# An inference step of a two-layer hybrid backbone: tensor-tensor work taken from POOL to DVE, and four adaLN segments of the second layer made in that layer

## The chip, the core and the metric

The kernel runs on one core of one Trainium2 chip. The metric is the device time of one execution in microseconds (us); the median of three timed runs of the kernel before is 1954.43 us (1951.92 to 1954.71). All times below are of that core. Its engines are PE (matrix multiplication), DVE and ACT (elementwise work on 128 partitions; DVE also reduces), POOL (GpSimd, elementwise too) and SP, which issues all of the kernel's DMAs.

## The reference, cut to what matters

512 latent tokens and 128 context tokens, 1024 channels, two layers (DEPTH), float32. In each layer a vector of six modulation segments is made from the conditioning vector and used for both norms and both residual additions:

```python
mod = jax.nn.silu(cvec) @ p['w_ada'] + p['b_ada']
sh1, sc1, g1, sh2, sc2, g2 = jnp.split(mod, 6, axis=-1)
h = rmsnorm(x, p['norm1_g']) * (1 + sc1) + sh1
out, k, v = mixer(h, p, rope, ctx_kv)       # pooling, gated conv and attention; three gates; w_o
x = x + g1 * out
h2 = rmsnorm(x, p['norm2_g']) * (1 + sc2) + sh2
ffn = (jax.nn.silu(h2 @ p['w_gate']) * (h2 @ p['w_up'])) @ p['w_down']
x = x + g2 * ffn
```

Latent and context tokens have their own conditioning vector (`c` and `c_ctx`), so that each segment exists twice. `w_ada` has 1024 x 6144 weights per layer.

## The kernel before

Channels lie on partitions, tokens on columns: a tensor of 1024 channels is eight chunks of 128 x 640 (KC = 8, TOK = 640), which PE works on in two halves of 320 columns. Float32 products are made of rounded parts: every operand is split into `hi` (ACT rounds it) and `lo` (an elementwise engine subtracts), and PE adds up hi*hi, lo*hi and hi*lo. So every weight block that arrives by DMA costs ACT one copy (L351) and one subtraction on DVE (L355) or POOL (L353), in `half_split`, and so does every activation (`split`, L297 to L301). A `Unit` is such a weight block; `stream` loads them in the order in which PE takes them.

The stages of a layer, in order: first norm; keys, values, queries, pooling and convolution projections with attention beside them ("attention stage"); 24 merges of a gate, a branch projection and their product (`gate`, L1484 to L1502, "gate stage"); the output projection `w_o` with the residual and the second norm (`residual`, `norm_chunk`); the FFN in four groups. Most FFN weight blocks go through `Pair` and `Seven`, which make a product of two 2 x 2 blocks by seven multiplications and need sums of weight blocks (`sums`, L446) and of activations (`combine`, L544). `hidden_of` (L1922 to L1931) turns the result into hidden activations, which a down-projection then takes.

The adaLN segments: in the first layer, segments 0 and 1 (shift and scale of the first norm) are made at the very start. All others come from `ada_back`: each 128-channel block of a segment is two jobs of 512 columns; a job loads 256 KB of `w_ada` into one of two buffers `p`, and DVE runs one reduction of 512 columns per conditioning vector (`ttr`, L756), which the profile shows as two instructions, a custom one and the read of its accumulator. The conditioning vectors stand in tiles `k`, which the keys of attention use before.

The order of all engines' instructions is written down by a plan: generators (tasks) yield operations with costs (L261 to L278) and a slack, and `_Order.run` takes for each engine the operation that is due first. For an operation that two engines can do (`dve_pool`) `_Order.push` takes the one that, by these costs, ends it first. On the chip each engine runs its list strictly in that order and waits on semaphores. `ttr` has the slack BACK (1e7 ns), so that the plan puts it where it believes DVE to be free; `quiet` keeps it out while a norm is made.

Names that the text uses: L353 and L355 weight subtractions; L446 sums of weight blocks; L902 the multiplication of a chunk by the norm's factor, L924 and L926 its affine step on ACT and DVE, L948 the subtraction that yields its low part; L849 the sum of squares; L651 the addition of a PSUM result to an accumulator in `Seven`; L300 and L301 the split of hidden activations and merged gates; L1489 and L1495 the products and sums of the merges; L885 and L1030 powers (x to -0.5), which POOL alone does.

## Time and profile before

| | |
|---|---|
| median of 3 runs | 1954.43 us (1951.92 to 1954.71) |
| profiled execution | 1951.29 us, its span 1949.2 us |
| PE busy | 1849.3 us (95%) |
| DVE busy | 1460.6 us (75%) |
| ACT busy | 795.3 us (41%) |
| POOL busy | 307.9 us (16%) |
| SP | issues the DMAs: 195.81 MB, mean 100 GB/s |

Stages of the profiled execution, by the places where the chain of waits changes its lines: start to 64 us; first layer's attention to 235.3, its gates to about 476 and output projection to 519.6, second norm to 585, FFN to about 990; norm between the layers to 1040; second layer's attention to 1200, gates and output projection to 1473.7, norm to 1538.2, FFN to 1929.2; the final norm to 1949.2.

How to read it: PE's busy time includes pipelined matmuls whose ends are modelled. An engine's wait is put down to what released it last. An idle engine off the path costs nothing, and a busy share of the whole span hides that the first layer has adaLN work and the second none.

### The profile page before, as it was taken

To read this page: it belongs to the slowest core of one execution; us is meant where nothing else is said; L and a number is where in the kernel's file an instruction comes from. 1 tells how busy PE (TensorE), PEld (TensorE's weight loads), DVE (VectorE), ACT (ScalarE), POOL (GpSimd) and SP (SyncE) were. 2 spreads that over 40 slices of the span, in tenths; PEclk is the share of its full clock that TensorE was granted. 3 is DMA by queue.
4 is the path that set the end of the run, shared out by engine and by line. 5 is a ranking of instruction groups with operands and counts; after the bars stand their busy time and mean duration, and the time that the engine had idled before them with its cause. 6 is when DMAs were issued, how large, how long until landed. Compare 5 with 4: busy or idle time off the path is not lost.

```text
span 1949.2 us, 31521 instructions
## 1 busy us (share of the span) xinstructions
PE 1849.3 (95%) x12427; PEld 1806.2 (93%) x12427; DVE 1460.6 (75%) x2529; ACT 795.3 (41%) x1396; POOL 307.9 (16%) x246
## 2 busy tenths in 40 slices
PE   6999999998989999999988999999998999999997
PEld 4889999998979999999988889999998899999997
DVE  7699778888889998997777996333347957768575
ACT  5476622222344242342454675222224534425244
POOL 3333000000341010100135320000004301001011
PEclk9999999999999999999999999999999999999998
DMA  8211144446314434433242100222241122222222
GB/s 303 77 35 40 39 151 158 169 161 227 114 33 133 155 112 159 136 129 107 69 161 60 35 29 33 77 82 76 76 141 55 52 90 76 87 76 79 84 71 71
DMA packets 76533, 195.81 MB, mean 100 GB/s; under 512 B 8801, under 2 KB 12897, under 8 KB 76385
## 3 DMA queue, kind: packets, MB, share of 16 engines
q1 hardware_dynamic: 76386, 193.81, 29.9%
q8 instruction: 97, 1.59, 0.3%
q14 instruction: 50, 0.41, 0.1%
HBM read 186.96 MB, written 5.51 MB: 99 GB/s over the span
## 4 chain that ended last, share of the span: by engine, by line
PE 63%; DVE 26%; issue 5%; DMA 3%; ACT 3%; POOL 1%; SPq 0%; DVEq 0%; ACTq 0%; POOLq 0%
PE ps L686 41%; PE ps L589 16%; DVE junk L756 5%; DVE wq L355 5%; DMA p<-in_w_ada 2%; DVE g L298 1%; PE ps L1209 1%; PE ps L1247 1%; PE ps L1227 1%; DVE u L446 1%; DVE g L301 1%; DVE g L948 1%; DVE st L1215 1%; DVE g L926 1%; PE ps L1682 1%
## 5 line engine op out<-in xcount | busy, mean ns | idle before, releaser
L686 PE MATMUL ps<-g,wq 128*128 128x320 f32 x7488 | 1153.9, 311 | 18.6 <-ACT g L300 10.1
L686 PEld LDWEIGHTS ps<-g,wq 128*128 128x128 f32 x7488 | 1112.7, 189 | 25.8 <-ACT g L300 11.7
L589 PE MATMUL ps<-g,wq 128*128 128x320 f32 x3360 | 502.7, 311 | 16.5 <-DVE z L651 13.9
L589 PEld LDWEIGHTS ps<-g,wq 128*128 128x128 f32 x3360 | 497.1, 189 | 21.1 <-DVE z L651 17.6
L355 DVE TENSOR_TENSOR wq<-wr,wq 128x512 fp32r<-128x512 f32 (+2 forms) x289 | 266.4, 922 | 157.3 <-ACT wq L351 156.1
L351 ACT CAST wq<-wr 128x512 fp32r<-128x512 f32 (+2 forms) x312 | 244.6, 784 | 311.9 <-PE ps L686 228.9
L1534 DVE SCALAR_TENSOR_TENSOR g<-ps,mod,g 128x128 f32<-128x128 f32 (+3 forms) x172 | 83.5, 522 | 120.7 <-PE ps L686 120.5
L756 DVE CUSTOM_DVE_ANT_0 junk<-p,k,vec 128x512 f32<-128x512 f32 x160 | 129.8, 811 | 29.5 <-DMA p<-in_w_ada 26.3
L351 ACT CAST wq<-u 128x512 fp32r<-128x512 f32 x160 | 98.3, 620 | 118.8 <-PE ps L589 61.9
L756 DVE CUSTOM_DVE_ANT_0 junk<-p,k,part 128x512 f32<-128x512 f32 x160 | 124.3, 777 | 19.2 <-DMA p<-in_w_ada 16.6
L355 DVE TENSOR_TENSOR wq<-u,wq 128x512 fp32r<-128x512 f32 x160 | 117.2, 737 | 16.5 <-ACT wq L351 16.5
L1484 ACT ACTIVATE t<-ps 128x640 f32<-128x640 f32 x32 | 22.6, 706 | 197.0 <-PE ps L686 197.0
L446 POOL TENSOR_TENSOR u<-u,wr 128x512 f32<-128x512 f32 x23 | 34.3, 1493 | 404.8 <-DVE u L446 403.4
L849 POOL TENSOR_TENSOR u<-u,t 128x320 f32<-128x320 f32 x11 | 14.8, 1351 | 429.2 <-ACT t L844 429.2
L353 POOL TENSOR_TENSOR wq<-wr,wq 128x1024 fp32r<-128x1024 f32 x23 | 57.6, 2505 | 109.2 <-ACT wq L351 99.2
L686 PE MATMUL ps<-g,g 128*128 128x320 f32 x192 | 46.7, 360 | 21.3 <-DVE g L948 18.6
L1217 ACT ACTIVATE p<-ps,st 128x640 f32<-128x640 f32 x64 | 50.9, 796 | 35.9 <-DVE st L1215 26.3
L924 ACT ACTIVATE g<-t,mod,gain 128x128 fp32r<-128x128 f32 (+4 forms) x96 | 50.9, 576 | 31.9 <-DVE gain L1695 14.6
L298 DVE TENSOR_TENSOR g<-ps,g 128x640 fp32r<-128x640 f32 (+1 forms) x68 | 54.9, 809 | 10.5 <-ACT g L297 9.9
L686 PEld LDWEIGHTS ps<-g,g 128*128 128x128 f32 x192 | 33.4, 212 | 30.1 <-DVE g L948 25.2
L902 POOL TENSOR_TENSOR t<-g,u 128x320 f32<-128x320 f32 (+1 forms) x41 | 53.8, 1320 | 39.8 <-ACT u L970 9.0
L297 ACT CAST g<-ps 128x640 fp32r<-128x640 f32 (+1 forms) x68 | 46.5, 686 | 26.5 <-PE ps L1227 21.9
(172 smaller groups left out, 1702.5 us busy)
## 6 DMA issues: line engine op xcount, KB each, us to landing
p<-in_w_ada SPq DMA_DIRECT2D x160, 256.0 KB, 2.8
wr<-in_w_in SPq DMA_DIRECT2D x76, 512.0 KB, 3.3
wr<-in_w_gate SPq DMA_DIRECT2D x44, 512.0 KB, 3.3
wr<-in_w_up SPq DMA_DIRECT2D x44, 512.0 KB, 3.3
wr<-in_w_down SPq DMA_DIRECT2D x48, 384.0 KB, 3.1
g<-in_w_ada SPq DMA_DIRECT2D x16, 512.0 KB, 7.2
wr<-in_w_br SPq DMA_DIRECT2D x32, 256.0 KB, 2.7
wr<-in_w_o SPq DMA_DIRECT2D x16, 512.0 KB, 4.3
```

Of the source, the lines that this page charges most:

```text
L298: yield dve(n, lambda: nc.vector.tensor_sub(lo, src, hi))
L351: yield act(n, lambda: nc.scalar.copy(hi, src), slack=WEIGHT)
L353: yield pool(n, lambda: nc.gpsimd.tensor_sub(lo, src, hi), slack=WEIGHT)
L355: yield dve(n, lambda: nc.vector.tensor_sub(lo, src, hi), slack=WEIGHT)
L446: f = lambda e: e.tensor_tensor(p[q], p[x], p[y], op=op)
L589: nc.tensor.matmul(out, lhsT=wt[q][:, k * P : k * P + P], rhs=x.get(t, lo, k), start=start and k == 0 and i == 0, stop=stop and k == 3 and ...
L686: nc.tensor.matmul(toks(ps, c0, n), lhsT=wt[:, c], rhs=xt[:, c0 : c0 + n], start=start and i == 0, stop=stop and i == 2,)
L756: return dve(n + 60, lambda: nc.vector.tensor_tensor_reduce(out=waste[:, :n], in0=w, in1=s, scale=0.5, scalar=start, op0=ALU.mult, op1=ALU ...
L902: f = lambda e: e.tensor_mul(t[:, :n], xk, r)
L924: nc.scalar.activation(out, sl, AF.Identity, bias=bias, scale=scale)
L1217: yield act(TOK + 140, lambda: nc.scalar.activation(pp, toks(ps), AF.Exp, bias=st[:, 0:1], accum_out=st[:, 1:2]))
L1534: yield dve(n, lambda: nc.vector.scalar_tensor_tensor(xs, toks(ps, s0, n), mods[l][:, v, seg * KC + m : seg * KC + m + 1], xs, op0=ALU.mul ...
```

## The change

1. Every operation that DVE or POOL could do (`dve_pool`) becomes one that DVE alone does (`dve_any`), and the places with a fixed share for POOL (`back` weight units, the first norm's multiplications, two of eight chunks of the final norm) go to DVE. POOL keeps the powers, the edge factors of the pooling mixer and memsets.
2. `ada_back` is started in each layer's gate stage: in the first layer it makes that layer's segments 2 to 5 and the second layer's segments 0 and 1 (48 blocks), in the second layer that layer's segments 2 to 5 (32 blocks). Before, all 80 blocks belonged to the first layer. The plan holds a norm until the two segments that it reads are made.

```diff
-    def dve_pool(n, f, **kw):
-        return _Op({"dve": 1.04 * n + 75, "pool": 2.2 * n + 100}, lambda e: f(ENG[e]), bias=BIAS, **kw)
+    def dve_any(n, f, **kw):
+        return dve(n, lambda: f(nc.vector), **kw)
...
-    def half_split(hi, lo, src, n, back=False):
+    def half_split(hi, lo, src, n):
         yield act(n, lambda: nc.scalar.copy(hi, src), slack=WEIGHT)
-        if back:
-            yield pool(n, lambda: nc.gpsimd.tensor_sub(lo, src, hi), slack=WEIGHT)
-        else:
-            yield dve(n, lambda: nc.vector.tensor_sub(lo, src, hi), slack=WEIGHT)
+        yield dve(n, lambda: nc.vector.tensor_sub(lo, src, hi), slack=WEIGHT)
...
-                yield dve_pool(n, f, slack=4.0 * WEIGHT)
+                yield dve_any(n, f, slack=4.0 * WEIGHT)
...
-    def ada_back(keys_free):
+    def ada_back(keys_free, todo):
...
-        todo = [(0, 2 * KC + (m + 0)) for m in range(4 * KC)] + [(1, m) for m in range(NADA)]
         jobs = [(l, m, q) for l, m in todo for q in range(2)]
...
         f = lambda e: e.tensor_mul(t[:, :n], xk, r)
-        if first:
-            yield pool(n, lambda: f(nc.gpsimd))
-        else:
-            yield dve(n, lambda: f(nc.vector)) if psum else dve_pool(n, f)
+        yield dve(n, lambda: f(nc.vector))
...
         yield h.made
+        for sg in (3 * which, 3 * which + 1):
+            yield ada_done[l][sg]
...
-        if k in (2, 5):
-            yield copied
-            yield pool(n, lambda: nc.gpsimd.tensor_mul(xk, xk, r_sb))
-        else:
-            yield dve(n, lambda: nc.vector.tensor_mul(xk, xk, r_ps))
+        yield dve(n, lambda: nc.vector.tensor_mul(xk, xk, r_ps))
...
-            bg = None
-            if l == 0:
-                bg = spawn(ada_back(att.done))
+            todo = [(l, m) for m in range(2 * KC, NADA)]
+            todo += [(l + 1, m) for m in range(2 * KC) if l + 1 < DEPTH]
+            bg = spawn(ada_back(att.done, todo))
```

The ten other uses of `dve_pool` change in the same way as the one in `sums`.

The first place is DVE's list at the first layer's second norm, where its second token half begins. Before (multiplication L902, affine step L926, subtraction L948; `msn` the mean squares, `t` the products):

```order
L883 TENSOR_SCALAR msn_84<-ps_5301 128x3
L902 TENSOR_TENSOR t_5324<-g_4627,ps_5301 128x320
L902 TENSOR_TENSOR t_5330<-g_4627,u_4630 128x320
L926 TENSOR_SCALAR g_4634<-t_5324,gain_76,mod_74 128x192
L926 TENSOR_SCALAR g_4634<-t_5324,gain_76,mod_74 128x128
L926 TENSOR_SCALAR g_4634<-t_5330,gain_76,mod_74 128x192
L948 TENSOR_TENSOR g_4632<-g_4634,g_4629 128x320
L926 TENSOR_SCALAR g_4634<-t_5330,gain_76,mod_74 128x128
L926 TENSOR_SCALAR g_4634<-t_5331,gain_76,mod_74 128x192
L948 TENSOR_TENSOR g_4632<-g_4634,g_4629 128x320
```

The same place after; the lines of the steps are now L897, L918 and L940:

```order
L878 TENSOR_SCALAR msn_84<-ps_5300 128x3
L897 TENSOR_TENSOR t_5322<-g_4614,ps_5300 128x320
L897 TENSOR_TENSOR t_5328<-g_4614,u_4617 128x320
L897 TENSOR_TENSOR t_5329<-g_4614,u_4617 128x320
L918 TENSOR_SCALAR g_4621<-t_5322,gain_76,mod_74 128x192
L918 TENSOR_SCALAR g_4621<-t_5322,gain_76,mod_74 128x128
L918 TENSOR_SCALAR g_4621<-t_5328,gain_76,mod_74 128x192
L940 TENSOR_TENSOR g_4619<-g_4621,g_4616 128x320
L897 TENSOR_TENSOR t_5347<-g_4614,u_4617 128x320
L918 TENSOR_SCALAR g_4621<-t_5328,gain_76,mod_74 128x128
L918 TENSOR_SCALAR g_4621<-t_5329,gain_76,mod_74 128x192
L940 TENSOR_TENSOR g_4619<-g_4621,g_4616 128x320
```

Before, DVE multiplied two of the eight chunks of this half and POOL the other six; after, all eight stand in DVE's list, three ahead of the first affine step and then one by one between the others.

The second place is DVE's list in the second layer's gate stage. Before (weight subtractions L355, products L1489, sums L1495, a merge's low part L301):

```order
L355 TENSOR_TENSOR wq_12564<-wr_12418,wq_12563 128x512
L1489 SCALAR_TENSOR_TENSOR t_12562<-t_12562,ps_12558 128x640
L1495 TENSOR_TENSOR u_12321<-u_12321,t_12562 128x640
L355 TENSOR_TENSOR wq_12596<-wr_12440,wq_12595 128x1024
L301 SCALAR_TENSOR_TENSOR g_12139<-u_12321,g_12137 128x640
L355 TENSOR_TENSOR wq_12656<-wr_12491,wq_12655 128x1024
```

After (L352, L1479, L1485 and L301 are the same steps; L752 is the reduction, `ISA` both its instructions):

```order
L1479 SCALAR_TENSOR_TENSOR t_12249<-t_12249,ps_12244 128x640
L752 ISA junk,mod_75<-p_12265,k_11994,part 128x512
L752 ISA mod_75 128x1
L1485 TENSOR_TENSOR u_11884<-u_11884,t_12249 128x640
L352 TENSOR_TENSOR wq_12289<-wr_12115,wq_12288 128x1024
L301 SCALAR_TENSOR_TENSOR g_11956<-u_11884,g_11954 128x640
L752 ISA junk,mod_75<-p_12265,k_12093,part 128x512
L752 ISA mod_75 128x1
L752 ISA junk,part<-p_12284,k_11953,vec 128x512
L752 ISA part 128x1
L752 ISA junk,part<-p_12284,k_12051,vec 128x512
L752 ISA part 128x1
```

Some six reductions now stand in each merge of the second layer, between the steps that the merge itself needs; before there were none.

## Rows read from the trace of the kernel before

**Rows 1.** The page, busy us of each engine (share of span), instructions
```profile
PE 1849.3 (95%) x12427; PEld 1806.2 (93%) x12427; DVE 1460.6 (75%) x2529; ACT 795.3 (41%) x1396; POOL 307.9 (16%) x246
```

**Rows 2.** Stages: stretch, length, each engine's busy us (instructions), clock, DMA share, GB/s
```profile
64.00:235.30 171.30, 163.78 (x1176) 159.26 (x1175) 145.93 (x251) 109.45 (x212) 48.27 (x47) 0.99 0.13 40
235.30:519.60 284.30, 275.84 (x1858) 273.60 (x1858) 225.70 (x458) 69.74 (x98) 19.89 (x10) 0.99 0.50 168
519.60:585.00 65.40, 54.08 (x333) 50.93 (x332) 58.76 (x88) 34.65 (x63) 30.00 (x23) 0.95 0.12 41
585.00:990.00 405.00, 390.18 (x2603) 384.82 (x2604) 362.54 (x712) 151.75 (x266) 41.31 (x28) 0.99 0.39 128
990.00:1040.00 50.00, 42.66 (x268) 40.32 (x266) 38.96 (x72) 26.57 (x53) 27.16 (x19) 0.93 0.33 106
1040.00:1200.00 160.00, 148.66 (x1055) 142.82 (x1056) 141.09 (x238) 103.12 (x203) 41.75 (x46) 0.99 0.13 39
1200.00:1473.70 273.70, 273.70 (x1870) 273.70 (x1869) 99.37 (x118) 68.34 (x94) 6.18 (x4) 1.00 0.26 87
1473.70:1538.20 64.50, 54.11 (x334) 50.78 (x334) 58.65 (x88) 34.62 (x63) 30.35 (x23) 0.94 0.13 42
1538.20:1929.20 391.00, 390.54 (x2643) 390.01 (x2643) 271.88 (x416) 161.09 (x283) 36.43 (x27) 0.99 0.24 76
```

**Rows 3.** PE's waits, first layer's gates: what waited, releaser: us, times, longest
```profile
PE ps L686 <- ACT g L300: 5.1, 1, 5.1
PE ps L686 <- DVE wq L355: 2.9, 4, 1.7
```

**Rows 4.** PE's waits in the first layer's FFN, same columns
```profile
PE ps L589 <- DVE z L651: 10.5, 11, 3.3
PE ps L686 <- ACT g L300: 4.8, 4, 2.0
```

**Rows 5.** AdaLN reductions, line L756: DVE busy by stretch; durations ns min/median/max
```profile
235.30:519.60 284.30, 137.45 (x340) 0.99 0.50 168
585.00:990.00 405.00, 119.10 (x300) 0.99 0.39 128
...
L756 DVE CUSTOM_DVE_ANT_0 junk<-p,k,vec x160: 736/752/2069, 258.5 to 891.7; 128x512 f32<-128x512 f32 x160
```

**Rows 6.** The chain that ended last: start us, length us, what
```profile
76.99 2.55 POOL wq L353
235.29 135.52 PE ps L686 x924
```

**Rows 7.** Groups, shapes apart: line, what, count, busy us, mean ns, idle before
```profile
L355 DVE TENSOR_TENSOR wq<-wr,wq 128x1024 fp32r<-128x1024 f32 x73 | 89.7, 1229 | 49.5 <-ACT wq L351 48.7
L353 POOL TENSOR_TENSOR wq<-wr,wq 128x1024 fp32r<-128x1024 f32 x23 | 57.6, 2505 | 109.2 <-ACT wq L351 99.2 <-DVE st L1220 8.8 <-POOL u L1383 0.7
L902 POOL TENSOR_TENSOR t<-g,u 128x320 f32<-128x320 f32 x33 | 37.6, 1144 | 27.1 <-ACT u L970 9.0 <-DVE g L926 6.2 <-ACT g L924 5.6
L1923 DVE SCALAR_TENSOR_TENSOR t<-t,t 128x640 f32<-128x640 f32 x40 | 46.3, 1157 | 7.2 <-ACT t L1922 7.2
L1489 DVE SCALAR_TENSOR_TENSOR t<-t,ps 128x640 f32<-128x640 f32 x32 | 26.1, 816 | 11.7 <-PE ps L686 11.7
L446 DVE TENSOR_TENSOR u<-wr,wr 128x512 f32<-128x512 f32 x23 | 22.9, 996 | 0.0
L446 DVE TENSOR_TENSOR u<-wr 128x512 f32<-128x512 f32 x33 | 22.6, 686 | 1.0 <-DMA wr<-in_w_up 0.7
L651 DVE TENSOR_TENSOR t<-t,ps 128x320 f32<-128x320 f32 x80 | 38.6, 482 | 6.1 <-PE ps L589 4.3
L1030 POOL TENSOR_TENSOR msz<-msz,mhalf 128x10 f32<-128x10 f32 x10 | 21.3, 2127 | 12.3 <-DVE msz L1028 12.3
```

**Rows 8.** Instructions in order of time, POOL's and DVE's: start us, us, what
```profile
371.81 2.42 POOL L1495 TENSOR_TENSOR u<-u,t 128x640 f32<-128x640 f32 x1 [27.25 <-DVE t L1489]
...
372.73 2.06 DVE L756 CUSTOM_DVE_ANT_0 junk<-p,k,vec 128x512 f32<-128x512 f32 x1
```

More of the change, by code (lines that the diff above doesn't have):

```diff
@@ L362, in tile_backbone, with __init__ @@
     class Unit:
-        def __init__(self, src, n=D, back=False, gate=None, big=False):
-            self.src, self.n, self.back, self.gate, self.big = src, n, back, gate, big
+        def __init__(self, src, n=D, gate=None, big=False):
+            self.src, self.n, self.gate, self.big = src, n, gate, big
             self.loaded, self.ready, self.placed = event(), event(), event()
@@ L386, in prepare @@
             s, raw = self.raw[0]
-            yield from half_split(self.hi[:, :n], self.lo[:, :n], raw[:, :n], n, self.back)
+            yield from half_split(self.hi[:, :n], self.lo[:, :n], raw[:, :n], n)
             RAW.put(s)
@@ L459, in free @@
             WQ.put(self.slot[q])
-    BACK_FROM, BACK_M = 2, 0
     SHIFT = 2000.0
@@ L470, in tile_backbone @@
             gate = go_weights[i] if l == 0 and i < 3 else None
-            plan.append(Unit(a[n][l, b], gate=gate, back=i >= max(BACK_FROM, 3 - 3 * l), big=i == 0))
+            plan.append(Unit(a[n][l, b], gate=gate, big=i == 0))
         MERGE = [(0, 0), (0, 1), (1, 0), (1, 1), (0, 2), (1, 2)]
@@ L474, in tile_backbone @@
         for m, b in MERGE:
-            plan.append(Unit(a["w_in"][l, B_G + b * KC + m], back=m < BACK_M and b < 2))
+            plan.append(Unit(a["w_in"][l, B_G + b * KC + m]))
             if b != 1:
@@ L543, in combine @@
                 for c in (slice(0, 2), slice(2, 4)):
-                    yield dve_pool(2 * HA, lambda e: e.tensor_sub(b[q][:, c], b[x][:, c], b[y][:, c]))
+                    yield dve_any(2 * HA, lambda e: e.tensor_sub(b[q][:, c], b[x][:, c], b[y][:, c]))
                 split_up.append(spawn(self.parts(q, b[q])))
@@ L849, in add @@
                     f = lambda e: e.tensor_add(self.acc[:, c], self.acc[:, c], sq[:, :n])
-                    yield dve_pool(n, f) if k < KC - 3 else dve(n, lambda: f(nc.vector))
+                    yield dve_any(n, f) if k < KC - 3 else dve(n, lambda: f(nc.vector))
                     TT.put(i)
@@ L1058, in rotary @@
         c = spawn(cosine())
-        yield dve_pool(LAT, lambda e: e.tensor_mul(sw[:, :LAT], sw[:, :LAT], rope.t[:, 1, :LAT]))
+        yield dve_any(LAT, lambda e: e.tensor_mul(sw[:, :LAT], sw[:, :LAT], rope.t[:, 1, :LAT]))
         yield c
@@ L1115, in one @@
                 yield dma(hi[r1, PAST:].bitcast(F32), hi[r0, PAST:].bitcast(F32), follow=True, done=d)
-                yield dve_pool(TOK, lambda v: v.tensor_sub(lo[r0, PAST:], z[r0, :], hi[r0, PAST:]))
+                yield dve_any(TOK, lambda v: v.tensor_sub(lo[r0, PAST:], z[r0, :], hi[r0, PAST:]))
                 yield dma(lo[r1, PAST:].bitcast(F32), lo[r0, PAST:].bitcast(F32))
@@ L1178, in one @@
                 yield act(TOK, lambda: nc.scalar.copy(q[r0, :], z[r0, :]))
-                yield dve_pool(TOK, lambda v: v.tensor_sub(q[r1, :], z[r0, :], q[r0, :]))
+                yield dve_any(TOK, lambda v: v.tensor_sub(q[r1, :], z[r0, :], q[r0, :]))
             for d in [spawn(one(e)) for e in range(2)]:
@@ L1368, in pool_mix @@
         lo, hi = 1, POOLW
-        yield dve_pool(POOLW, lambda e: e.tensor_add(cur[:, lo:hi], u[:, lo:hi], u[:, lo - 1 : hi - 1]))
+        yield dve_any(POOLW, lambda e: e.tensor_add(cur[:, lo:hi], u[:, lo:hi], u[:, lo - 1 : hi - 1]))
         step = 1
@@ L1372, in pool_mix @@
             lo, hi = lo + step, hi - step
-            yield dve_pool(POOLW, lambda e: e.tensor_add(
+            yield dve_any(POOLW, lambda e: e.tensor_add(
                 nxt[r, lo:hi], cur[r, lo - step : hi - step], cur[r, lo + step : hi + step]))
@@ L1495, in gate @@
                 f = lambda e: e.tensor_add(acc, acc, t)
-                yield dve_pool(TOK, f) if b == 1 else dve(TOK, lambda: f(nc.vector))
+                yield dve_any(TOK, f) if b == 1 else dve(TOK, lambda: f(nc.vector))
                 TT.put(i)
@@ L1922, in hidden_of @@
         yield act(TOK, lambda: nc.scalar.activation(t, c.x, AF.Tanh, scale=0.5))
-        yield dve_pool(TOK, lambda e: e.scalar_tensor_tensor(t, t, 1.0, c.x, op0=ALU.add, op1=ALU.mult))
+        yield dve_any(TOK, lambda e: e.scalar_tensor_tensor(t, t, 1.0, c.x, op0=ALU.add, op1=ALU.mult))
         TT.put(c.xslot)
         yield c.c22
-        yield dve_pool(HA, lambda e: e.tensor_mul(t[:, HA:], t[:, HA:], c.y))
+        yield dve_any(HA, lambda e: e.tensor_mul(t[:, HA:], t[:, HA:], c.y))
         ZZ.put(c.yslot)
```

## The prediction

> **What bounds the kernel now.** I read the page's busy times first, then the stage table, then who waited for whom on PE. PE is busy for 1849.3 of 1949.2 us and DVE for 1460.6 [rows 1], so only some 100 us of PE idle can be won at all. The stage table shows where they are [rows 2]. The two layers do the same matmuls, so each stage of the first has a twin without adaLN work in the second. The first layer's gate stage with its output projection takes 284.3 us with 8.5 of PE idle, the twin 273.7 with none. The first layer's FFN takes 405 us with 14.8 idle, the twin 391.0 with 0.5. Beside them stand the two attention stages (7.5 and 11.3 idle), the two norms between mixer and FFN (11.3 and 10.4) and the norm between the layers (7.3), where DVE is busy for 78 to 91%.
>
> What PE waits for in the first layer is DVE, or ACT behind it. At the gate stage's end one wait of 5.1 us stands for the last merge, and 2.9 us go to weight halves [rows 3]. In the FFN PE waits 10.5 us for accumulators to be read out (L651) and 4.8 for the hidden tiles (L300) [rows 4]; 3.3 of the 10.5 end just as this stretch begins, and the second layer has the same 3.3. The adaLN instructions keep DVE busy for 137.5 and 119.1 us in these two stretches, and for nothing in the second layer [rows 5].
>
> **The change, part by part.** *AdaLN moved.* Before, 160 jobs of two halves (320 custom reductions) run in the first layer, 153 reductions up to the end of the gates, 17 in the output projection and 150 in the FFN, by the order on DVE. After, the first layer has 96 jobs: 144 to 146 reductions up to the end of the gates, 16 in the projection, 30 in the FFN, the last of them beside the first group's down-projection. The 128 others stand among the second layer's merges 4 to 22 of 24.
>
> FFN of the first layer: 150 reductions become 30. With the twin as the floor, its idle can fall from 14.8 to 0.5. I leave a fifth of it (30 of 150), about 3: a gain of 12, bounds 8 and 14.8. The gate stage of the first layer keeps its load, as adaLN still runs beyond its end: a gain of 1 of the 8.5, bounds -3 and 4.
>
> Gate stage of the second layer: 64 jobs in a stage whose DVE is busy for 99.4 of 273.7 us. At the cost of before (137.5 and 119.1 us for the 320) the 128 reductions add 103 us, which gives DVE 202 of 274, against 225.7 of 284.3 in the first layer. The ends of the unknown are 0 (in the first layer PE ran for 135.5 us from 235.3 on without a stop, with reductions from 258.5 on [rows 5, 6]) and 8.5 (all that the first layer's stage lost). The 5.1 us there came at the end, with reductions still in front of the last merge. Here the last one stands two merges earlier, and DVE can catch up. I take 3. The same stage gets 64 pairs' loads and four loads of the conditioning vectors on SP; the first layer moves 168 GB/s in this stage and no wait of PE there names a DMA. No new wait is late on the chip: the second layer's first two segments are done beside the first of four groups of the first layer's FFN and read after the fourth, and its other four end before the output projection needs the last but one of them.
>
> *POOL's work to DVE.* POOL is busy for 307.9 us [rows 1]; the power operations (21.3 for the ten of L1030 [rows 7]), the edge factors and memsets stay, some 45 us, and about 263 move. On DVE such work takes 1229 ns instead of 2505 for 1024 columns, and 482 instead of 1144 for 320, thus 0.42 to 0.49 of POOL's time: 263 becomes 110 to 129 us, I say 118. By stage, from POOL's busy time less what stays: 15 in the first attention, 14 in the second, 12.6 in each norm, 10 in the norm between the layers, 17 in either FFN, 8 at the start.
>
> Against it stands what POOL costs DVE now. At 371.8 a POOL addition ran for 2.42 us and DVE's reduction that began under it took 2.06 us, where the median is 0.752 [rows 5, 8]: it ended 0.56 us after POOL did. That is 1.31 us lost by DVE for an instruction that DVE does itself in 0.82. It shows in groups with two SBUF operands and not in those that read PSUM: L1923 takes 1157 ns where L1489 with the same 640 columns takes 816, and L446 takes 996 for one pair of operands and 686 for another [rows 7]. These two groups alone lose 40 x 0.34 + 23 x 0.31 = 21 us; if every moved POOL instruction cost DVE 0.54 of its time (1.31 of 2.42), it would be 142. I take 100. So DVE's total hardly changes: 1460.6 + 118 - 100 = 1479, between 1437 and 1558.
>
> The Trainium skill ("SBUF — State Buffer", section on SBUF's two separate sides) says that GpSimd and a VectorE instruction with two SBUF inputs take one port pair in turn, each for its whole length. The row of 2.06 us agrees. By that rule alone the return would lie towards the 142, and DVE would be 24 us lighter than now.
>
> What is left is where POOL's length stood on the path. In a norm, DVE is busy for 58.8 of 65.4 us [rows 2], and its order for the second token half is three multiplications first, then by chunk affine, affine, subtract, multiply. The added multiplications cost 12.6 us. The stalls there should give back 0.54 x 30 = 16, a net 3.6, of which I count 2.5 for each of the two norms (bounds -8 and 6). For the norm between the layers 1 (bounds -5 and 3), for the start 1 (bounds -4 and 4). In attention 15 and 14 us against a return of half of the POOL time that goes (about 35 and 30, so 19 and 16 by the 0.54): I take 0 for each, bounds -6 and 5; there POOL's weight halves of 2.5 us also stood ahead of the power operation that the head norms wait for, as the chain has it at 77 us [rows 6]. The tail: two more multiplications of 0.48 on DVE per four chunks, in place of POOL's, 0.5 lost.
>
> *Sum.* 12 + 1 - 3 + 2 x 2.5 + 1 + 1 + 0 - 0.5 = 16.5 us. The profiled execution took 1951.3 us (span 1949.2 and 2.1 around it), 3.1 under the median of 1954.4. It becomes 1934.8, or 1938 by the median; I say **1937**. The terms are independent: the root of the summed squares of their distances to the bounds is 20 us towards slower and 11 towards faster. Half of each gives this case's own range, 1931 to 1947.
>
> **Rivals.** *The second layer's gates pay what the first's paid.* DVE runs its queue in order, and a reduction whose operand has not landed holds the weight halves behind it. If this costs 8.5 and the end of the stage shifts too, the loss is 10 instead of 3: 1944. For it: the first layer's stage did just that at a load only a tenth higher. Against: the two free merges at the end. Chance 0.14.
>
> *The FFN's idle is not adaLN's.* Its waits name L651 and L300, not the reductions; if POOL's instructions made it, or the new order keeps it, the 12 go to 2: 1947. Against: the twin has nearly as much POOL work (36.4 against 41.3 us) and no idle. Chance 0.06.
>
> *DVE is overloaded where it was full (slower).* The mechanism: DVE's durations stay what they are, and the added 12.6 us stand in norms whose DVE has only 6.7 and 5.9 us free, the 15 and 14 in attention stages that are 85 and 88% full. Each norm then grows by at least 6, with the order's stalls 8, and each attention stage by about half of what it gets, 7; with 5 between the layers and 4 at the start that is 39 lost against 10 won: 1983. It decides from the point at which DVE gets back less than a third of the 118. In its favour: DVE's shares, and the subtractions that PE waits for are behind the added multiplications. Against it: the row of 2.06 us. Chance 0.09.
> The Trainium skill ("Perfetto Trace Analysis", section on optimizing Scalar/DVE operations) counsels giving work to GPSIMD when DVE is saturated, but adds that the shared read port may undo it. Its first half is this rival; the trace speaks for its second half.
>
> *The new order is worse in the attention stages alone.* Both are filled by a plan that prices DVE too low (it reckons a reduction of 512 columns at 670 ns, whose first instruction alone takes 752 [rows 5]). At -6 each the sum is 4.5: 1950. Chance 0.11.
>
> **Chances and range.** Forecast 0.60, the rivals 0.14, 0.06, 0.09 and 0.11. Less than 0.2% (3.9 us either way, 1950.5 to 1958.3) can't be told from no change here. The forecast, the first two rivals and half of the last fall below that: 0.84, of which I move 0.03 to no change, since several small losses may come together. Faster 0.81, same 0.10, slower 0.09. The range for 8 in 10 is 1926 to 1951; above it lie the slower rival and the worst of the order.
>
> **What would show it.** In the profile after: POOL busy near 45 us and DVE between 1437 and 1558; the longest reduction of 512 columns near its median, not 2.06 us; L1923 near 816 ns. The first layer's FFN within 3 us of the second's. In the second layer's gate stage some 100 us of reductions and PE idle of up to 4. Norms of 62 to 64 us. A DVE total above 1540, a norm longer than 65.4 us, or a second gate stage over 282 us would make it wrong.

## The result, and the profile after

The changed kernel takes 1878.88 us (median of four runs, 1877.90 to 1883.69) against 1954.32 us (four runs, 1951.92 to 1954.71) of the kernel before: a ratio of 0.9621, 95% interval 0.9603 to 0.9640. It is 75 us faster where 16.5 were forecast, and 47 us under the lower end of the range. The direction was right, the size wrong by a factor of 4.6.

The page's busy times answer to [rows 1]:

```profile
PE 1827.1 (97%) x12427; PEld 1794.6 (95%) x12427; DVE 1424.9 (76%) x2663; ACT 816.6 (43%) x1437; POOL 40.1 (2%) x79
```

DVE took over what POOL needed some 263 us for, and its total is *lower* than before: 1424.9 instead of 1460.6. PE's busy time fell by 22.2 us for the same 12427 matmuls, so it had held time in which PE worked at less than its full rate. The mean granted clock of the whole span rose from 0.983 to 0.990 of 2.4 GHz; by an estimate from these two figures (0.017 of 1949.2 us less 0.010 of 1881.7) that is at most some 14 us, and no run here shows what the rest is.

The stage table of the kernel after, cut as [rows 2] as nearly as its chain of waits allows (stretch, length, busy us and instructions of PE, weight load, DVE, ACT and POOL, granted clock, DMA share, GB/s):

```profile
60.00:225.90 165.90, 162.32 (x1183) 158.86 (x1182) 143.37 (x255) 116.82 (x223) 15.65 (x33) 1.00 0.14 46
225.90:508.50 282.60, 272.86 (x1831) 270.09 (x1831) 214.75 (x450) 69.60 (x97) 0.00 (x0) 0.99 0.50 163
508.50:562.10 53.60, 49.34 (x331) 47.61 (x329) 48.13 (x97) 35.06 (x67) 1.70 (x2) 0.99 0.14 45
562.10:957.00 394.90, 393.08 (x2655) 391.98 (x2655) 288.91 (x515) 157.11 (x274) 0.00 (x0) 0.99 0.30 95
957.00:1000.00 43.00, 39.52 (x262) 37.64 (x262) 33.79 (x78) 27.49 (x55) 7.58 (x4) 0.96 0.32 105
1000.00:1149.40 149.40, 148.81 (x1086) 145.87 (x1086) 135.89 (x241) 109.03 (x211) 9.46 (x31) 1.00 0.13 42
1149.40:1415.40 266.00, 264.43 (x1798) 263.38 (x1797) 188.81 (x381) 67.85 (x95) 0.00 (x0) 1.00 0.47 155
1415.40:1469.00 53.60, 49.34 (x331) 47.57 (x329) 48.15 (x97) 35.06 (x67) 1.70 (x2) 1.00 0.14 45
1469.00:1860.30 391.30, 390.76 (x2650) 390.24 (x2651) 267.38 (x450) 161.97 (x285) 0.00 (x0) 1.00 0.24 77
```

Each norm is 11 to 12 us shorter, the first FFN 10 (18.2 when both are cut at the same matmuls, as in the table further down), the attention stages shorter too; the first gates are nearly as long as they were. In the gates some of the gain is work moved, since the new plan runs some gate matmuls already beside attention: cut at the same matmuls as in the table further down, the second layer's stretch has 1797 of them instead of 1864, the first layer's 1831 instead of 1852. Attention and gates of a layer are therefore best read as one.

What a norm's gain consists of shows when only its first 269 matmuls are windowed, first before, then after:

```profile
518.60:569.00 50.40, 43.71 (x269) 41.24 (x269) 42.76 (x67) 25.87 (x47) 25.31 (x20) 0.93 0.10 32
```

```profile
508.50:548.20 39.70, 39.02 (x269) 38.48 (x268) 34.23 (x75) 26.26 (x51) 1.70 (x2) 1.00 0.12 41
```

Of the 10.7 us, 6.0 were PE's idle time (6.7 before, 0.7 after). The other 4.7 stood inside PE's busy time: the granted clock averaged 0.93 there, 2.4 GHz less a part of the stretch at 1.2, and is 1.00 now that PE hardly pauses. By an estimate from this row, a mean of 0.93 over 50.4 us is 3.5 us of full clock lost, so that the clock can account for at most that much of the 4.7. DVE is busy for 34.2 us instead of 42.8, although it has 75 instructions instead of 67: of POOL's 20 it took over 18, and some ten of its own stand elsewhere or on ACT now.

PE's waits in the first gates (what waited, releaser: us, times, longest) answer to [rows 3]:

```profile
PE ps L682 <- DVE wq L352: 5.0, 6, 1.1
PE ps L682 <- ACT g L300: 4.2, 1, 4.2
```

and in the first FFN to [rows 4]:

```profile
PE ps L585 <- DVE wq L352: 2.4, 1, 2.4
PE ps L682 <- DVE g L301: 1.6, 2, 1.3
PE ps L682 <- ACT g L300: 0.2, 1, 0.2
```

In these rows the first gates wait as before, the FFN far less. The adaLN reductions by stretch (first gates, first FFN, second gates) and their durations (ns, min/median/max) answer to [rows 5], and the longest, 754 ns instead of 2069, to [rows 8]: no reduction is held up any more.

```profile
225.90:508.50 282.60, 122.90 (x324) 0.99 0.50 163
562.10:957.00 394.90, 22.69 (x60) 0.99 0.30 95
1149.40:1415.40 266.00, 97.06 (x256) 1.00 0.47 155
...
L752 DVE CUSTOM_DVE_ANT_0 junk<-p,k,vec x160: 741/752/754, 249.5 to 1348.9; 128x512 f32<-128x512 f32 x160
```

The chain of waits at 73 to 84 us, where [rows 6] had POOL's weight half of 2.55 us, holds PE alone (start us, length us, what):

```profile
73.21 4.96 PE ps L682 x33
78.18 0.56 PE ps L1029 x5
78.74 4.84 PE ps L682 x33
```

Four groups, shapes apart (count, busy us, mean ns), answer to [rows 7]:

```profile
L1913 DVE SCALAR_TENSOR_TENSOR t<-t,t 128x640 f32<-128x640 f32 x40 | 32.8, 821 | 6.1 <-ACT t L1912 6.1
L443 DVE TENSOR_TENSOR u<-wr,wr 128x512 f32<-128x512 f32 x40 | 27.5, 688 | 0.7
L897 DVE TENSOR_TENSOR t<-g,u 128x320 f32<-128x320 f32 x42 | 19.9, 485 | 0.0
L1020 POOL TENSOR_TENSOR msz<-msz,mhalf 128x10 f32<-128x10 f32 x10 | 22.1, 2210 | 118.7 <-DVE msz L1018 106.3 <-DVE st L1210 12.4
```

The product of the hidden activations went from 1157 to 821 ns, the weight sums from 996 to 688, although DVE has more of them (40 instead of 23). The powers stay on POOL at their old length.

### The profile page after: what moved, and what is told of

Read it like the earlier page. It is cut to its first block, busy times and chain, and to the rows that moved or that the text cites. A ratio compares the mean times of both kernels' runs of the same rounds, so it can differ in the third digit from the quotient of the medians.

```text
span 1881.7 us, 31312 instructions
## 1 busy us (share of the span) xinstructions
PE 1827.1 (97%) x12427; PEld 1794.6 (95%) x12427; DVE 1424.9 (76%) x2663; ACT 816.6 (43%) x1437; POOL 40.1 (2%) x79
## 4 chain that ended last, share of the span: by engine, by line
PE 68%; DVE 17%; DMA 8%; issue 4%; ACT 2%; POOL 0%; SPq 0%; DVEq 0%; POOLq 0%; ACTq 0%
PE ps L682 35%; PE ps L585 25%; DMA p<-in_w_ada 7%; DVE junk L752 5%; DVE wq L352 4%; PE ps L1199 2%; PE ps L1237 2%; PE ps L1217 2%; DVE u L1485 1%; DVE t L1479 1%; PE ps L1672 1%; DVE g L555 1%; PE ps L1010 1%; DVE g L298 0%; DVE g L301 0%
## 5 line engine op out<-in xcount | busy, mean ns | idle before, releaser
L682 PEld LDWEIGHTS ps<-g,wq 128*128 128x128 f32 x7488 | 1106.9, 188 | 24.2 <-DVE wq L352 10.2
L352 DVE TENSOR_TENSOR wq<-wr,wq 128x512 fp32r<-128x512 f32 (+2 forms) x312 | 278.0, 891 | 46.6 <-ACT wq L351 45.5
L752 DVE CUSTOM_DVE_ANT_0 junk<-p,k,vec 128x512 f32<-128x512 f32 x160 | 120.0, 750 | 49.2 <-DMA p<-in_w_ada 46.0
L752 DVE CUSTOM_DVE_ANT_0 junk<-p,k,part 128x512 f32<-128x512 f32 x160 | 120.0, 750 | 27.4 <-DMA p<-in_w_ada 23.8
L352 DVE TENSOR_TENSOR wq<-u,wq 128x512 fp32r<-128x512 f32 x160 | 109.3, 688 | 22.5 <-ACT wq L351 21.8
L642 ACT COPY t<-ps 128x320 f32<-128x320 f32 x80 | 34.2, 427 | 75.7 <-PE ps L585 75.7
L916 ACT ACTIVATE g<-t,mod,gain 128x320 fp32r<-128x320 f32 (+5 forms) x108 | 55.6, 572 | 5.7 <-DVE t L897 3.3
L1205 DVE TENSOR_REDUCE st<-ps 128x1 f32<-128x640 f32 x64 | 52.2, 815 | 3.9 <-PE ps L1199 3.6
L300 ACT ACTIVATE g<-u 128x640 fp32r<-128x640 f32 x16 | 11.8, 739 | 94.9 <-DVE u L1485 94.9
L301 DVE SCALAR_TENSOR_TENSOR g<-t,g 128x640 fp32r<-128x640 f32 x44 | 36.2, 823 | 17.7 <-ACT g L300 17.7
L1199 PE MATMUL ps<-k,g 128*128 128x320 f32 x256 | 48.9, 313 | 0.3 <-ACT p L1207 0.2
L647 DVE TENSOR_TENSOR t<-t,ps 128x320 f32<-128x320 f32 x80 | 38.7, 484 | 10.3 <-PE ps L585 7.8
## 6 DMA issues: line engine op xcount, KB each, us to landing
wr<-in_w_down SPq DMA_DIRECT2D x48, 384.0 KB, 3.1
```

Source lines behind the costliest of these rows:

```text
L352: yield dve(n, lambda: nc.vector.tensor_sub(lo, src, hi), slack=WEIGHT)
L682: nc.tensor.matmul(toks(ps, c0, n), lhsT=wt[:, c], rhs=xt[:, c0 : c0 + n], start=start and i == 0, stop=stop and i == 2,)
L752: return dve(n + 60, lambda: nc.vector.tensor_tensor_reduce(out=waste[:, :n], in0=w, in1=s, scale=0.5, scalar=start, op0=ALU.mult, op1=ALU ...
L916: nc.scalar.activation(out, sl, AF.Identity, bias=bias, scale=scale)
L1199: nc.tensor.matmul(toks(ps, c0, n), lhsT=qs, rhs=kt[:, c0 : c0 + n], start=j == 0, stop=j == 1)
L1205: yield dve(TOK, lambda: nc.vector.tensor_reduce(st[:, 0:1], toks(ps), axis=AX.X, op=ALU.max, negate=True))
```

## The experiments

Each was run with the kernel before on the same chip (medians there 1951.8 to 1953.1 us). Stage lengths in us, each cut at the same matmul of the program (last matmul of attention, first of a norm's statistics, first and last of the FFN's seven products); the last product of the second FFN to the end takes 45 to 47 us in every kernel of the table. A gate stage that is shorter behind an attention stage that is longer can be matmuls moved from one into the other; the sum of the two is then what counts:

| | before | after | POOL alone | adaLN alone | before's plan, POOL's work on DVE | after, true costs | true costs, one layer | before, true costs |
|---|---|---|---|---|---|---|---|---|
| start, attention | 235.1 | 225.9 | 223.8 | 235.9 | 233.0 | 227.0 | 226.6 | 237.4 |
| gates, w_o | 283.6 | 282.6 | 279.1 | 284.5 | 282.5 | 265.6 | 265.6 | 271.3 |
| norm | 50.4 | 39.7 | 39.7 | 50.2 | 44.6 | 39.7 | 39.7 | 50.0 |
| FFN | 400.8 | 382.6 | 389.5 | 384.0 | 397.5 | 380.8 | 381.2 | 385.1 |
| its down tail, norm, attention | 229.9 | 218.6 | 217.2 | 231.8 | 223.5 | 217.2 | 307.2 | 272.7 |
| gates, w_o | 273.1 | 266.0 | 263.4 | 277.0 | 273.1 | 263.4 | 231.3 | 235.7 |
| norm | 49.4 | 39.7 | 39.7 | 49.8 | 44.6 | 39.7 | 39.7 | 49.4 |
| FFN | 381.1 | 379.7 | 379.7 | 381.2 | 378.6 | 379.7 | 380.9 | 378.6 |

**One half of the change each.** First POOL's work on DVE with all 80 adaLN blocks left in the first layer:

```diff
-            todo = [(l, m) for m in range(2 * KC, NADA)]
-            todo += [(l + 1, m) for m in range(2 * KC) if l + 1 < DEPTH]
-            bg = spawn(ada_back(att.done, todo))
+            todo = [(0, m) for m in range(2 * KC, NADA)] + [(1, m) for m in range(NADA)]
+            bg = spawn(ada_back(att.done, todo)) if l == 0 else None
```

> The first half of the change alone: POOL's tensor-tensor work goes to DVE, all 80 adaLN blocks stay in the first layer. Theory A (POOL's work was the cost: norms 20, attention with start about 20 to 28 of the 75 us): 1900 to 1912 us, norms near 40 us from the statistics to the first FFN product as in the changed kernel, the first FFN still some 10 us over the second. Theory B (the adaLN move is the larger part, and gave the norms and attention room as well): over 1925 us.

1880.60 us, ratio 0.9635 (0.9612 to 0.9659): 72.5 us, nearly the whole gain, and 19 us under the lower end of what theory A expected.

Then the kernel before with adaLN split between the layers, and nothing else:

```diff
-    def ada_back(keys_free):
+    def ada_back(keys_free, todo):
...
-        todo = [(0, 2 * KC + (m + 0)) for m in range(4 * KC)] + [(1, m) for m in range(NADA)]
...
+        for sg in (3 * which, 3 * which + 1):
+            yield ada_done[l][sg]
...
+            todo = [(l, m) for m in range(2 * KC, NADA)]
+            todo += [(l + 1, m) for m in range(2 * KC) if l + 1 < DEPTH]
+            bg = spawn(ada_back(att.done, todo))
```

> The second half alone: adaLN split between the layers, POOL keeps its tensor-tensor work. By the terms of the prediction (12 from the first FFN, 1 from its gates, 3 lost in the second layer's gates): 1942 to 1946 us, norms and attention stages as before. Theory B: under 1925 us. If the second layer's gates pay what the first's paid under POOL's stalls: 1948 to 1952 us.

1942.66 us, ratio 0.9950 (0.9930 to 0.9970): 10.5 us, as the prediction's adaLN terms had it (12 + 1 - 3 = 10). By stage it is 16.8 won in the FFN and 3.9 lost in the second gates. The halves don't add up: 72.5 + 10.5 = 83 against 75.

**POOL put to work again, for nothing.** Three kernels take the changed one and let POOL repeat instructions of DVE into a tile that nobody reads. The lists of the other engines stay word for word what they were, and in the traces of the three no engine but POOL waits for one of the added instructions, so DVE instructions that take longer are held up. (`idle` is the tile that nobody reads.) In the norms, 36 multiplications of 320 columns:

```diff
+        if not first and k >= 2:
+            def twin():
+                yield pool(n, lambda: nc.gpsimd.tensor_mul(idle[:, :n], xk, r))
+            spawn(twin())
         yield dve(n, lambda: f(nc.vector))
```

> The changed kernel, with 36 multiplications of 320 columns more on POOL in the three norms: each repeats one that DVE does, into a tile that nobody reads. The lists of PE, DVE, ACT and SP stay word for word those of the changed kernel. Port theory (a POOL instruction holds up DVE instructions with two SBUF operands for what is left of its length): DVE busy rises by 15 to 30 us in the norms and the time by 10 to 22 us, to 1889 to 1901. Latency theory (POOL only was slow to deliver, and the plan's order is better without it): the time stays within 2 us of the changed kernel's, since nobody waits for these results.

1903.01 us, ratio 0.9744 (0.9721 to 0.9767): 24 us slower than the changed kernel, for POOL work that nobody waits for. Groups of this run:

```profile
L901 POOL TENSOR_TENSOR idle<-g,u 128x320 f32<-128x320 f32 x36 | 36.9, 1024 | 12.6 <-ACT u L970 10.3
...
L898 DVE TENSOR_TENSOR t<-g,u 128x320 f32<-128x320 f32 x42 | 30.5, 736 | 0.0
...
L924 DVE TENSOR_SCALAR g<-t,gain,mod 128x192 f32<-128x192 f32 x10 | 6.1, 614 | 0.0
```

and the group of the changed kernel that answers to the last:

```profile
L918 DVE TENSOR_SCALAR g<-t,gain,mod 128x192 f32<-128x192 f32 x10 | 3.7, 374 | 0.0
```

DVE's multiplication rises from 485 to 736 ns. So does its affine step, 374 to 614, which has one wide operand and two of one column, not two tensors. The first norm's 269 matmuls:

```profile
506.00:553.60 47.60, 42.00 (x269) 40.04 (x268) 41.37 (x75) 26.70 (x51) 13.78 (x14) 0.96 0.10 34
```

That is 7.9 of the 10.7 us which the change had won there. DVE's total grows by 21.4 us (1424.9 to 1446.3), the time by 24: the hold-up reached the end in full. The time is 2 us above the expected range.

Beside the weight subtractions of the attention stages, two half-width copies of each of 23:

```diff
+        if twin:
+            def second():
+                for c in (slice(0, HA), slice(HA, 2 * HA)):
+                    yield _Op({"pool": 0.0}, lambda e: nc.gpsimd.tensor_sub(idle, src[:, c], hi[:, c]))
+            spawn(second())
         yield dve(n, lambda: nc.vector.tensor_sub(lo, src, hi), slack=WEIGHT)
```

> The changed kernel, with two subtractions of 320 columns more on POOL (results read by nobody) for each of the 23 weight blocks of the attention stages whose low part POOL made before. The other engines' lists stay word for word. Port theory: DVE busy in the two attention stages rises by 20 to 35 us and the time by 5 to 20 us, to 1884 to 1899. Latency theory: within 2 us of the changed kernel, except for the wait of a weight buffer on POOL's reading.

1893.95 us, ratio 0.9700 (0.9678 to 0.9722): 15 slower, with DVE's total up by 17.6. The first attention takes 6.4 us longer, the second 7.5.

All of it together, 178 instructions (36 in the norms, 46 beside weights, 16 in the first norm, 80 beside the FFN's weight sums; the last by this edit):

```diff
                 f = lambda e: e.tensor_tensor(p[q], p[x], p[y], op=op)
+                if q in ("s1", "s2"):
+                    def twin():
+                        yield _Op({"pool": 0.0}, lambda e: nc.gpsimd.tensor_tensor(
+                            idle, p[x][:, :HA], p[y][:, :HA], op=op))
+                    spawn(twin())
```

> The changed kernel with 178 instructions of 320 columns on POOL whose results nobody reads: the 36 of the norms, the 46 of the weight blocks, 16 in the first norm, 80 with the sums of weight blocks in the two FFNs, some 200 us of POOL in all (before: 263 more than after). The other engines' lists stay word for word. Port theory: DVE busy up by 80 to 120 us; 24 us in the norms and 15 in attention as in the two twins before, 3 to 6 at the start, 5 to 25 in the FFNs: 1926 to 1950 us. If the FFN has room on DVE for all of it: 1920.

1933.86 us, ratio 0.9904 (0.9880 to 0.9927), 55 us slower than the changed kernel:

```profile
PE 1852.4 (96%) x12427; PEld 1811.5 (94%) x12427; DVE 1496.8 (77%) x2663; ACT 818.2 (42%) x1437; POOL 242.0 (13%) x257
```

POOL has 202 us more, DVE 72 (80 to 120 were expected), and PE is busy for 25 us more with the same matmuls. The norms are back at the length that they had before (50.6 and 49.7 us); start and first attention lose 20.3, norm between the layers and second attention 15.5. The two FFN stretches, from their first product to the next norm's statistics, hold 80 of the instructions; first in the changed kernel, then here:

```profile
548.20:956.75 408.55, 403.15 (x2717) 401.00 (x2716) 302.56 (x535) 165.66 (x290) 0.00 (x0) 0.99 0.30 94
1455.10:1860.30 405.20, 401.08 (x2714) 399.36 (x2713) 281.28 (x471) 170.76 (x301) 0.00 (x0) 1.00 0.24 76
```

```profile
577.10:986.60 409.50, 403.67 (x2717) 400.99 (x2717) 313.96 (x535) 165.48 (x290) 40.55 (x37) 0.99 0.29 94
1508.20:1913.60 405.40, 401.04 (x2714) 399.33 (x2714) 291.37 (x471) 170.37 (x301) 40.05 (x37) 1.00 0.24 76
```

DVE is held up there for 11.4 and 10.1 us, and the stretches grow by 1.0 and 0.2. So hold-up costs its full length outside the FFNs (the other 50 of the 72 us cost 54) and almost nothing in them, where 5 to 25 us were expected. It fits that DVE has room in the FFNs (it is busy for 74 and 69% of the two stretches in the changed kernel) and little in the norm (86%) and the attention stages (86 and 91%).

**Which property of POOL's work holds DVE up.** The norm experiment again, but POOL fills the tile with zeros, 144 times, and so reads nothing:

```diff
+                for _ in range(4):
+                    yield _Op({"pool": 0.0}, lambda e: nc.gpsimd.memset(idle, 0.0))
```

> The changed kernel with 144 memsets of 320 columns on POOL in the norms, four where e3_norm_twin had a multiplication; they read nothing. The other engines' lists stay word for word. If POOL holds up DVE by reading two operands from SBUF: within 3 us of the changed kernel (1876 to 1883), DVE busy unchanged. If any POOL instruction that writes to SBUF holds it up: 1887 or more.

1879.52 us, ratio 0.9625 (0.9609 to 0.9641), the changed kernel's time:

```profile
PE 1826.0 (97%) x12427; PEld 1793.9 (96%) x12427; DVE 1426.8 (76%) x2663; ACT 817.3 (44%) x1437; POOL 94.4 (5%) x223
```

54 us more on POOL, 1.9 more on DVE. The 1.9 all lie in one kind of DVE instruction: the multiplication of two tensors keeps the length that it has in the changed kernel (485 ns), while the affine step of 128 columns goes from 341 ns (the last line, of the changed kernel) to 432.

```profile
L898 DVE TENSOR_TENSOR t<-g,u 128x320 f32<-128x320 f32 x42 | 19.9, 483 | 0.0
L925 DVE TENSOR_SCALAR g<-t,gain,mod 128x128 f32<-128x128 f32 x12 | 5.2, 432 | 0.0
```

```profile
L918 DVE TENSOR_SCALAR g<-t,gain,mod 128x128 f32<-128x128 f32 x12 | 4.1, 341 | 0.0
```

So what costs the time is not that POOL is busy: its instructions that read two tensors hold up both kinds of DVE instruction, its fills the affine step alone, and that too little to show in the time. POOL instructions that read one tensor were not tried.

**Moved work at its old place.** The kernel before with its own plan, where each tensor-tensor instruction that the plan gave to POOL is issued on DVE at the place that it had:

```diff
-ENG = {"act": nc.scalar, "dve": nc.vector, "pool": nc.gpsimd}
+ENG = {"act": nc.scalar, "dve": nc.vector, "pool": nc.vector}
...
-            yield pool(n, lambda: nc.gpsimd.tensor_sub(lo, src, hi), slack=WEIGHT)
+            yield pool(n, lambda: nc.vector.tensor_sub(lo, src, hi), slack=WEIGHT)
...
```

(and the two other fixed places in the same way.)

> The kernel before with its own plan and adaLN place: each tensor-tensor instruction that the plan gave to POOL is issued on DVE, at the place in DVE's list that its turn on POOL had. The lists of PE, ACT and SP are word for word those before. Theory A1 (POOL's holding up of DVE is the cost): nearly all of the gain of moving POOL's work, 1880 to 1900 us. Theory A2 (the plan, once DVE alone is to be had, writes a better order and gives ACT 20 us more): DVE is overloaded at these places, 1930 us or more.

1923.51 us, ratio 0.9851 (0.9837 to 0.9866): 28 us won, between the two expectations. DVE's total is 1427.9: 1460.6 + 118 - 1427.9 = 151 us of hold-up went away. (118 is the prediction's estimate; here it can be measured, since DVE's list is that of before with 167 instructions more, and by the mean times of their groups these take 117 us.) Yet 43 us more (1923.51 against 1880.60) come only when the plan knows that DVE does the work. They are spread over nearly all stages: norms 4.9 each, first FFN 8, start and first attention 9, second layer's attention and gates together 16. In the last the plan for DVE alone has also moved PE's work: 1518 matmuls stand in the attention stretch instead of 1453, and PE idles there for 4.5 us instead of 14.2.

**The norms' multiplications open to POOL again.**

```diff
-        yield dve(n, lambda: f(nc.vector))
+        yield dve(n, lambda: f(nc.vector)) if psum or first else dve_pool(n, f)
```

> The changed kernel with the norms' multiplications open to POOL again (as before: the plan chooses between DVE and POOL, 36 go to POOL). Port theory, with e3_norm_twin at 1903: POOL's holding up of DVE costs as in the twins, and DVE is spared 36 multiplications: 1893 to 1905 us. If the slow delivery counts as much as the hold-up: 1908 us or more. If neither counts: 1879.

1890.97 us, ratio 0.9691 (0.9677 to 0.9706), 2 us under the range of the port theory and 12 above the changed kernel. With 36 multiplications on POOL, DVE has work taken away and is yet busy 8 us longer (1433.0); the norms take 46.5 us instead of 39.7.

**Is it ACT's share?** The new plan gives ACT 21 us more than before. A penalty on ACT in the plan, to put the split of the work between DVE and ACT back:

```diff
-    BIAS = {"dve": 0.0, "act": 0.0, "pool": 0.0}
+    BIAS = {"dve": 0.0, "act": 500.0, "pool": 0.0}
```

(and this bias also on the affine step that either engine can do.)

> The changed kernel with DVE and ACT sharing the either-engine work as before the change: a bias of 500 ns on ACT in the plan leaves DVE 53 scalings and 65 affine steps (58 and 59 before the change, 40 and 41 after it). If the plan's handing of some 20 us of DVE's work to ACT is a large part of what the re-written plan gives: 1895 to 1915 us. If it is the order and the end of the hold-up: 1877 to 1886.

1881.71 us, ratio 0.9634 (0.9609 to 0.9659): no difference in the whole. With ACT at 795.6 us, as before the change, DVE is at 1438.5; this gives a second figure for the hold-up that went, 1460.6 + 118 - 1438.5 = 140 us.

**The plan's price of a reduction.** The first gates kept their length in the change, and their chain of waits is full of DVE waiting for a load `p<-in_w_ada`. The plan prices a reduction at 670 ns (1.04 x 572 + 75; the trace has 752 + 83) and puts it right behind the landing that it reckons with. So DVE meets reductions whose operand is not there, with weight halves queued behind. Two numbers in the changed kernel, a price of 836 ns and 1.2 us of distance from the landing:

```diff
             yield d
+            yield 1200.0
...
-        return dve(n + 60, lambda: nc.vector.tensor_tensor_reduce(
+        return dve(n + 220, lambda: nc.vector.tensor_tensor_reduce(
```

> A version meant to be better: the changed kernel with the adaLN reduction at 836 ns in the plan (its two instructions take 835 on the chip, the plan says 670) and each job's reductions 1.2 us later than the plan takes its load to land. If DVE's waits for adaLN loads (70 us, and 10 us of PE idle in the first layer's gates) are what is left: 1864 to 1874 us. If spreading adaLN into the FFN costs as much there: 1877 to 1886.

1862.86 us, ratio 0.9542 (0.9528 to 0.9557): 16 us faster than the change, 1 under the expected range, and the best of all versions. The two numbers were changed together; which of them did it was not tested. DVE's idle time ahead of reductions until their load has landed falls, after and then here (us, times):

```profile
  DMA p<-in_w_ada: 69.8, 50
```

```profile
  DMA p<-in_w_ada: 37.8, 23
```

and the first gates have no PE idle left, where they had 9.7 us (18 of their matmuls also stand in the attention stage now, which is 1.1 us longer):

```profile
227.00:492.60 265.60, 265.60 (x1813) 265.60 (x1813) 187.56 (x370) 68.88 (x96) 0.00 (x0) 1.00 0.47 154
```

It holds 244 reduction instructions there and 140 in the FFN, against 324 and 60: with the true price the plan puts more of them where DVE has room.

**The same with all adaLN in the first layer** (the edits of the last and of the first experiment):

```diff
+            yield 1200.0
...
+        return dve(n + 220, lambda: nc.vector.tensor_tensor_reduce(
...
+            todo = [(0, m) for m in range(2 * KC, NADA)] + [(1, m) for m in range(NADA)]
```

> The true adaLN cost in the plan (as in e8_true_cost, 1863 us) and POOL's work on DVE, but all 80 adaLN blocks in the first layer again. If the split is worth nothing beside the other half: 1860 to 1867 us. If the first FFN then pays (90 jobs or more in it): 1870 to 1885.

1919.78 us, ratio 0.9831 (0.9809 to 0.9853): both expectations missed. With the true price the plan spreads the reductions so thin that the last runs at 1103 us. The second layer's keys need the tiles `k` that hold the conditioning vectors (chain of waits: start us, length us, what):

```profile
1051.58 53.31 PE ps L682 x363
...
1110.03 4.56 DMA k<-k
```

The keys are loaded after that, and the stretch from the FFN's end to attention's end takes 307.2 instead of 217.2 us; 32 come back in the gates. Beside the true price the split is thus worth 57 us; beside the old price it was worth 2 (1880.60 against 1878.88), which the runs of the two kernels don't tell from nothing.

**And in the kernel before**, the two numbers alone:

```diff
+            yield 1200.0
...
+        return dve(n + 220, lambda: nc.vector.tensor_tensor_reduce(
```

> The kernel before with only the plan's adaLN cost and delay of e8_true_cost; POOL keeps its work, all adaLN in the first layer. If DVE's waits for adaLN loads cost 8 us in the first gates whatever POOL does: 1940 to 1947 us, less what more adaLN in the FFN costs. If POOL's hold-up is what makes adaLN late: no change, 1949 to 1956.

1928.57 us, ratio 0.9877 (0.9856 to 0.9897), below both expected ranges. 12.3 us are won in the first gates and 15.7 in the first FFN. The 42.8 lost up to the end of the second attention (272.7 for 229.9) and the 37.4 won in the gates behind it are mostly one thing, gate matmuls moved (1708 instead of 1452 stand in the first of the two stretches); together the two stretches lose 5.4.

## Why the prediction was right and wrong

*Hold-up by POOL: right in kind, undersized.* The term was the return of "100" between 21 and 142. Two kernels that divide the work between DVE and ACT as before, the one exactly and the other nearly, give 150 and 140. The one row that showed the mechanism, the reduction of 2.06 us [rows 8], scaled to 142, and that was nearly exact; 100 was a hedge towards groups with few affected instructions. By the rule of the Trainium skill ("SBUF — State Buffer", section on SBUF's two separate sides) the return was to lie towards the 142, and the runs agree.

*The step that failed most: from DVE's balance to time, in an order that was taken to stay.* The prediction set hold-up lost against work added, us for us, in the order of before. A new order had no term in the sum; it stood there only as a rival that loses. The terms for POOL's half (2 x 2.5, 1, 1, 0 and -0.5) make 6.5 us. Measured, the same exchange with the instructions at their old places won 28, and the plan that is written for DVE alone won 43 more: the term that was put at nothing is the largest of all. At the old places us for us came out in the whole (150 back for 117 added is 33, and 28 were won), so there the miss is the return of 100. By stage 10.7 and 9.7 came per norm where 2.5 stood, 10.2 for the start with the first layer's attention and gates, and 18.4 for the norm between the layers with the second layer's attention and gates.

The first layer's second norm shows both parts. The balance of its DVE work was right: 16 back for 12.6 added was forecast, and with the moved instructions at their old places DVE is busy for 54.07 us with 109 instructions where it was for 58.76 with 88, so some 17 came back. But this made the first 269 matmuls 5.8 us shorter (50.4 to 44.6) and not 2.5. The other 4.9 are the new plan's: in the changed kernel's stretch of 53.6 us DVE has 97 instructions, among them 14 affine steps instead of 20, the others standing at other places or on ACT.

Where hold-up falls decides its price: 21.4 us of it in the norms cost 24, 17.6 beside the attention's weights cost 15, 50 outside the FFNs cost 54, and 21.5 in the FFNs cost 1.2. Added work stands in the plan; that it is cheap because the plan sets it where DVE is free fits the 43 us but is not shown.

*"Only some 100 us of PE idle can be won at all": false as a bound.* PE's idle time fell from 99.9 to 54.6, its busy time by another 22.2. Busy time holds what PE loses while its matmuls run at the lower clock, as the norm's window shows (0.93 to 1.00, by the estimate above at most 3.5 of the 4.7 us). A mean granted clock under 1.00 in a stretch of [rows 2] was the sign: 0.95, 0.93 and 0.94 stood in just the three stretches that gained most for their length.

*AdaLN moved: right in the main.* 12 forecast for the first FFN, 18.2 measured for both halves and 16.8 for this one alone, over the upper bound of 14.8. That bound was PE's idle time in the stretch of [rows 2]; cut as in the table, the stretch had 19.0 us of idle before and has 4.9 after, and PE's busy time gave the other 4.1. The first gates were to gain 1 and gained 0.95, but that is luck: they have 21 matmuls fewer, some 3 us at 0.15 us each (282.6 us for 1831), and PE idles there for 9.7 us instead of 8.5. The second gates were to lose 3: by themselves 3.9, and 2.6 more in the changed kernel than with POOL's half alone; PE idles 1.6 us there (4 allowed for), and the 97.06 us of reductions are the 100 foretold. That either half of the change removes much of the FFN's loss (16.8 and 11.3, together 18.2) was in no term. Of the 11.3, the end of the hold-up alone gave 3.3 (400.8 to 397.5) and the new plan the other 8.

*Rivals.* An overloaded DVE, the slower one, was to decide from a return of less than a third of the 118; it returned more than all of it. The advice that it rested on, to give work to GPSIMD when DVE is saturated (the Trainium skill, "Perfetto Trace Analysis", section on optimizing Scalar/DVE operations), is refuted for this kernel by the run with multiplications opened to POOL (1890.97), and its own warning on the read port is borne out. Second gates that pay 8.5, an FFN idle of other cause and a worse order in attention did not happen. (The share for faster was summed a little low: 0.60, 0.14, 0.06 and half of 0.11 make 0.855, not 0.84.)

*Signs.* POOL 40.1 us (45 foretold), the longest reduction 754 ns, L1913 821 ns (816), the first FFN within 3 us of the second (382.6 and 379.7): as foretold. DVE at 1424.9 lies under the foretold 1437 to 1558, and the norms at 53.6 us under the 62 to 64.

*Left open:* what in the re-written plan wins the 43 us over the same instructions at their old places. ACT's share is not it. Part of the gain stands where gate matmuls moved beside the second attention, but no run holds those at their old places with the rest of the new plan. That the plan had reckoned POOL's slots at POOL's length, and set whatever follows accordingly late, is likely and was not tested.

## What to carry to other kernels

Judge a helper engine by what it blocks, not by what it takes off: 263 us of POOL work held DVE up for 140 to 150 and saved it 118. Price hold-up of the engine that feeds the bound one at full value in stages where it is nearly full (86 to 91% busy here), and near nothing where it has room (69 and 74%). When work moves between engines and a planner writes the order anew, give the new order a term of its own: here it was the larger one (43 us against 28). Read a granted clock below 1.00 in a stage as time to be won beside its idle time. Give a planner the durations of the trace (its price for a reduction, with a delay behind the load, won 16 us here), but ask anew what then ends late: the same two numbers without the split cost 39 us (1919.78 against 1880.60).

## What the runs showed of the hardware

- DVE is held up by POOL instructions that read two tensors (36 multiplications, 36.8 us: DVE +21.4) and hardly by ones that only write (144 fills, 54 us: DVE +1.9).
- What is held up depends on both sides. Beside POOL's multiplications DVE's multiplication of two tensors went from 485 to 736 ns and its affine step (one wide operand and two of one column, 192 columns) from 374 to 614. Beside POOL's fills the multiplication stayed (483), and the affine step of 128 columns went from 341 to 432.
- PE's granted clock averaged 0.93 in the norm whose PE paused for 6.7 us and 1.00 in the same norm with 0.7 us of pauses. PE was busy for 4.7 us less, of which the clock is at most 3.5 by the estimate above.
